# A two-layer hybrid encoder trunk: another order of the output product, low parts and score matmuls issued elsewhere, Fourier matmuls over 128 rows

## The chip, the core and the metric

The kernel runs on one core of a Trainium2 chip. The metric is device time in microseconds of one execution of the whole program. The kernel before was run three times; the time compared is the median. One further execution was recorded by the hardware profiler, and every row quoted here comes from that record. Its columns name the engines as the profile does: PE is the matrix engine, PEld its weight loads, DVE the vector engine, ACT the scalar engine, POOL the engine that issues the accumulating transfers, SP the one that issues the plain loads.

## What is computed

Two layers, each a half-step gated feed-forward block, a mixer of two parallel branches, and a second half-step feed-forward block; a norm at the end. Shapes: 512 tokens, width 1024, inner feed-forward width 2816, 8 heads of 64, all in 32-bit floats.

```
def mixer(h, w_in, gate_bias, rpb, w_na_out, w_f_out, w_o):
    z = h @ w_in                      # q, k, v (512 each), uf (512), ga, gf (1024 each)
    y_na = neighbourhood_attention(q, k, v, rpb) @ w_na_out
    y_f = fourier_mix(uf) @ w_f_out   # real part of a 2-D DFT over positions and channels
    g_na = sigmoid(ga + gate_bias[0])
    g_f = sigmoid(gf + gate_bias[1])
    return (g_na * y_na + g_f * y_f) @ w_o

x = x + 0.5 * swiglu(rms_norm(x, n1), ffn1_w_in, ffn1_w_out)
x = x + mixer(rms_norm(x, nm), ...)
x = x + 0.5 * swiglu(rms_norm(x, n2), ffn2_w_in, ffn2_w_out)
```

Neighbourhood attention works on a grid of 8 rows by 64 columns; a block of 16 query columns sees a band of 32 key columns, so a block's scores are 128 queries by 256 keys.

## The kernel before

**Arithmetic.** Every 32-bit product is made of three passes over rounded parts: high by high, high by low, low by high. A weight tile therefore comes as a raw tile (`raw`, loaded by DMA), a high part (`whi`, made on ACT, line 194 or negated on line 192) and a low part (`wlo`, raw minus high, made on DVE, line 201 or 199). PE takes the two products with `whi` first (lines 351 and 352) and the one with `wlo` last (line 354). Large products are done by a seven-product scheme over 2 by 2 blocks: products m1 to m7 of combined activations with combined weight blocks a, b, c, d. Combined weights are formed in three ways: while a tile is loaded (the POOL queue adds a second block into it, line 155), on DVE (line 187), or, once a tile has served one product, by a POOL transfer that adds another block for the next product (`then`, line 211).

**Stages.** Each layer has a feed-forward stage, a mixer stage and a feed-forward stage. The mixer of layer 1 lies at about 310 to 626 us of the span, that of layer 2 at about 1275 to 1570 us. In the mixer the order of work is written out by hand: on DVE, ACT and PE instructions are issued as the program lists them, from the last part of the feed-forward block before it to the line that closes that regime, ahead of the last gate blocks; behind it, and for the loads throughout, a scheduler that works with estimated times decides the order, unless a call pins an instruction.

**Mixer, in order.** Projections of v and u; q of head pair 0; the Fourier transform over positions (`four_pos`: per 128 output rows six matmuls and one small one, line 1174, that adds the middle row held in `ux`); projections of k and q; then eight attention steps. Step i (`att_step`) does the output of step i-2 (`att_out`), the transposes and splits of step i-1 (`att_trans`, lines 1280 and 359) and the scores of step i (`att_scores`): 12 matmuls of 64 rows on line 1246, two heads at a time, then on DVE the bias and running minimum (line 1255), on ACT the exponentials (line 1262), the division (lines 1268 and 1271). A head pair takes two steps, i even and i odd. Between the steps stand the Fourier transform over channels (`four_ch`, small matmuls on lines 1197 and 1203), projections, and the ten steps of `f_fill` (the Fourier branch's output product; PE tile `ef`, evacuated by ACT and DVE, lines 1362 to 1365, tile `fs`). PSUM has eight banks for all of it, handed out in turn.

From step 5 on the gates' weights are prepared by calls placed by hand: `ws.high()` makes the next item's high part, `ws.low()` the next low part. Then the gate blocks run (`gate_block`, products into A, B, C), with the attention's output product (`n_rows`, PE tile `ps`) between them; `t12` is an activation sum built on DVE in four additions (lines 1555, 1557, 1585, 1589).

**The end of the mixer** multiplies by W_o: seven products into the banks wA, wB, wC, with activation sums m1 to m7 built from the gated branches. The order of products and that of the weights must agree; the latter is `ORDER_W`, line 34. In `strassen`, lines 235 to 242, weights of product 5 then take block a by a POOL transfer, and product 3's are a sum of d and b on DVE. Between the products x is updated (`put`, line 1671) and transposed for the next norm (tile `tr`, line 439).

**The loads.** `Raw.load` issues the plain load on SP and, for a combined tile, the accumulating transfer on POOL. Issue on each queue is in order: a transfer that waits holds those behind it.

Of the kernel before, what the change touches and what calls it, by code (L numbers as in the profile page):

```python
# [14 lines left out]
ALU = mybir.AluOpType  # L15
AX = mybir.AxisListType

P = 128
# [12 lines left out]
AHEAD = 2  # L31
ORDER = (1, 5, 2, 6, 7, 3, 4)
ORDER_0 = (1, 2, 5, 6, 7, 3, 4)
ORDER_W = (5, 1, 2, 6, 7, 3, 4)
FETCH = (8, 4)
BAND = (0, 1, 3, 4)
HALF = T // 2
KC = HALF + 2
# [57 lines left out]
def encoder_kernel(  # L96
# [47 lines left out]
    class Raw:  # L144
# [3 lines left out]
        def load(self, parts=1):  # L148
            if self.t is None:
                self.t = raw_pool[0](self.n)  # L150
                for c in range(0, self.n, self.n // parts):
                    cs = slice(c, c + self.n // parts)
                    nc.sync.dma_start(out=self.t[:, cs], in_=wst[GRAN_AT[self.key]][:, cs])
                if self.plus:
                    G.dma_start(out=self.t, in_=wst[GRAN_AT[self.plus]][:, 0 : self.n], accum_op=ALU.add)  # L155

    class Item:
        def __init__(self, raw, add=None, neg=False, stage=0, parts=1, pieces=1, then=None, minus=None, kept=False):
# [54 lines left out]
    def stage_items():  # L213
        items, st = [], 0

        def add(*a, **k):
            items.append(Item(*a, stage=st, **k))

        made = {}

        def strassen(s, name, idx, sizes, order, dma=False):
            r = made.setdefault((s, name("a"), idx), {}) if dma and len(order) < 7 and order[0] > 2 else {}
            for q, q2 in () if r else (("a", None), ("b", None), ("c", "a"), ("d", "c")):
                r[q] = [
                    Raw((s, name(q), idx, g), n, q2 and (s, name(q2), idx, g)) for g, n in enumerate(sizes)
                ]
            d2 = [Raw((s, name("d"), idx, g), n) for g, n in enumerate(sizes)]
            for m in order:
                for g in range(len(sizes)):
                    a, b, c, d = [r[q][g] for q in "abcd"]  # L230
                    if m == 1:
                        add(a, neg=True)
                    elif m == 2:
                        add(b)
                    elif m == 3:
                        add(d, None if dma and order is not ORDER_W else b)
                    elif m == 4:
                        add(d2[g])
                    elif m == 5:
                        add(d, then=a.key if dma else None)  # L240
                    elif m == 6:
                        add(d, None if dma else a, then=b.key if dma and order is not ORDER_W else None)
                    else:
                        add(c)

        def out_sizes(c):
            return (1024, 512) if c == 0 else (1024, 1024)

        def ffn(s):
            first = not items  # L250
            for g in range(4):
                add(Raw((s, "cl", g)), parts=2 if first and g < 2 else 1, pieces=2 if first and g == 0 else 1)
            for j in range(NB):
                order = (1, 2, 5, 6, 7, 3, 4) if s == (0, 1) and j == 0 else (1, 5, 6, 2, 7, 3, 4)
                strassen(s, lambda q: q, j, (1024, 1024), order)
            for order in ((1,), (2,), (5, 6, 7, 3), (4,)):
                for c in range(3):
                    strassen(s, lambda q: "o" + q, c, out_sizes(c), order)

        for l in range(L):  # L260
            ffn((l, 1))
            st += 1
            s = (l, 0)
            two = (1024, 1024)
            for g in VG:
                add(Raw((s, "v", g)), kept=g == VG[0])
            for g in range(3):
                add(Raw((s, "up", g), UC * len(UK[g]), (s, "uq", g)))
            for g in range(2):
                add(Raw((s, "un", g)), minus=(s, "um", g))  # L270
            for g in range(8):
                add(Raw((s, "qk", g)))
            for i in range(2):
                add(Raw((s, "fp", i), 1024, (s, "fq", i)))
# [12 lines left out]
        return items  # L287
# [676 lines left out]
    def stage_mixer(l, norm, nxt):  # L964
# [199 lines left out]
            return t  # L1164

        def four_pos():
            alt = fc[0:34, C_K : C_K + KC]
            for gp in range(3):
                cs = slice(gp * P, (gp + 1) * P) if gp < 2 else slice(HALF, UC)
                ps = bank()  # L1170
                to = ps[0 : cs.stop - cs.start, 0:KC]
                for b in range(2):
                    mm3(to, ue[b][:, 0, cs], ue[b][:, 1, cs], dfs[:, 0, b, 0:KC], dfs[:, 1, b, 0:KC], b == 0, False)
                PE.matmul(to, ux[0][0:34, cs], alt, start=False, stop=True)
                if gp == 2:
                    cx.append(low_rows(ps, "cx", 32))
                    continue
# [13 lines left out]
        def four_ch():  # L1191
            px = bank()
            for gp in range(2):
                a = fc[:, C_ALT + 4 * gp : C_ALT + 4 * gp + 4]
                for z in range(2):
                    PE.matmul(px[0:4, 0:KC], a, ce[gp][:, z, :], start=gp == 0 and z == 0, stop=False)
            PE.matmul(px[0:4, 0:KC], fc[0:36, C_X4 : C_X4 + 4], cx[0][0:36, 0:KC], start=False, stop=True)
            p64.append(low_rows(px, "p64", 64, (32,)))
            for gp in range(2):
                ps = bank()  # L1200
                to = ps[:, 0:KC]
                mm3(to, fc[:, C_COS : C_COS + P], fc[:, C_COS + P : C_COS + 2 * P], ce[gp][:, 0, :], ce[gp][:, 1, :], True, False)
                PE.matmul(to, fc[0:36, C_X + gp * P : C_X + gp * P + P], cx[0][0:36, 0:KC], start=False, stop=True)
                split(pf[gp][:, 0, :], pf[gp][:, 1, :], to)
                ps = bank()
                to = ps[:, 0:HALF]
# [1 line left out]
                split(qf[gp][:, 0, :], qf[gp][:, 1, :], to)  # L1208

        o, q, k, bms = [], {}, {}, {}  # L1210

        def proj_q(hp):
            q[hp] = hilo("q")
# [14 lines left out]
        def bias_for(hp):  # L1228
            bms[hp] = []
            for e in range(2):  # L1230
                res = mp.tile([P, 3, 256], F32, tag="bm", name=nm("bm"), bufs=4)
                nc.sync.dma_start(out=res, in_=near[l, 2 * hp + e])
                bms[hp].append(res)

        def att_scores(i, after):
            hp, pr = divmod(i, 2)
            (qh, ql), (kh, kl) = q[hp], k[hp]
            ps = [bank(), bank()]
            for jj in range(2):
                j = 2 * pr + jj  # L1240
                ks = slice(BAND[j] * 64, BAND[j] * 64 + 256)
                qs = slice(j * P, (j + 1) * P)
                for i, (a, b) in enumerate(((qh, kh), (qh, kl), (ql, kh))):
                    for e in range(2):
                        r = slice(64 * e, 64 * e + 64)
                        PE.matmul(
                            ps[e][:, jj * 256 : (jj + 1) * 256], a[r, qs], b[r, ks], start=i == 0, stop=i == 2
                        )
            s_ = [tmp(s="s"), tmp(s="s")]
            nmx = sp.tile([P, 4], F32, tag="nmx", name=nm("nmx"), bufs=4)  # L1250
            sm = sp.tile([P, 4], F32, tag="sm", name=nm("sm"), bufs=4)
# [54 lines left out]
                r = slice(64 * e, 64 * e + 64)  # L1306
                V.tensor_tensor(ol[r], pv[e], oh[r].bitcast(F32), ALU.subtract)

        sc, pt_ = {}, {}

        def att_step(i, then=None, before=None, last=None):
            if 0 <= i - 2 < 8:
                att_out(i - 2, pt_.pop(i - 2))
            if then:
                then()
            if 0 <= i - 1 < 8:
                pt_[i - 1] = att_trans(sc.pop(i - 1))
            if before:
                before()
            if i < 8:  # L1320
                sc[i] = att_scores(i, last)

# [201 lines left out]
        for _ in range(4):  # L1524
            next(f_rows)
        ws.high()
        next(f_rows)
        att_step(6, ws.low)
        for _ in range(5):
            next(f_rows)  # L1530
        ws.high()
        att_step(7, ws.low, ws.prep_one)
        next(block)
        ws.high()
        ws.low()
        next(block)
        next(block)
        ws.high()

        B = {(i, j): [z[i].bitcast(F32)[:, :, j * 256 : (j + 1) * 256] for z in (hx, lx)] for i in range(2) for j in range(2)}  # L1540

# [22 lines left out]
            split(hx[0][:, :, 256:512], lx[0][:, :, 256:512], t12)  # L1564

        next(first)
        att_step(8, ws.low)
        next(block)
        next(first)
        t12 = next(first)  # L1570
# [11 lines left out]
        acts[5] = low(h1, t12, "t1")  # L1582
        ws.high()
        ws.low()
        V.tensor_tensor(t12, t12, B[1, 1][0], ALU.add)
        next(block_1)
        ws.high()
        ws.low()
        V.tensor_tensor(t12, t12, B[1, 1][1], ALU.add)
        next(block_1)  # L1590
        h2 = high(t12, "t2")
# [42 lines left out]
        w = [ws.next(), ws.next()]  # L1634
        merge(1, ga1, gf1, w)
        m10, m11 = ga1
        a2 = parts(m10, "m2")
        pb = pair("wB")
        product(pb, a5, K4, True)
        put(pb, 1, 1, -1)  # L1640
        a6 = combo(m00, m00, m11, ALU.add, "m6")
        pa = pair("wA")
        product(pa, a1, K4, True)
        put(pa, 0, 0, -1)
        V.tensor_tensor(m01, m01, m11, ALU.subtract)
        a7 = parts(m01, "m7")
        a3 = parts(m11, "m3")
        pc = pair("wC")
        product(pc, a2, K4, True)
        put(pc, 0, 0, 1)  # L1650
        nxt.squares(0, 0)
        product(pa, a6, K4, False, again=True)
        put(pa, 0, 1, -1)
        a4 = combo(m10, m10, m00, ALU.subtract, "m4")
        product(pa, a7, K4, False, again=True)
        put(pa, 1, 1, 1)
# [232 lines left out]
```

## Time and profile before

| quantity | value |
|---|---|
| median of three runs | 1905.83 us |
| lowest and highest | 1903.82 and 1906.01 us |
| the profiled execution's own time | 1903.99 us |
| its span, first to last instruction | 1902.2 us |
| PE busy in the span | 1874.4 us (99%) |
| DVE, ACT, POOL busy | 1513.3, 1163.3, 172.9 us |
| mean granted PE clock | 0.997 |

The span lies 1.8 us under the execution's time, and that lies 1.84 us under the median of the runs. PE is idle for about 28 us of the span, hence a change can shorten the program either by closing some of this idle time or by making PE's busy work take less. A row of a timeline gives start, duration of one instruction (or of the group), engine, line, operation, output<-input, and in brackets the idle time ahead of it with what ended it. Since PE overlaps neighbouring matmuls, the cost of one is the distance from its start to the next start and not the duration that its row shows.

### The profile page before, as it was taken

What the parts mean: (1) busy time and instruction counts of PE and PEld (TensorE: products, weight loads), DVE (VectorE), ACT (ScalarE), POOL (GpSimd) and SP (SyncE); (2) the same over time, 40 slices, a digit from 0 to 9 for tenths busy, and PEclk for the clock granted to TensorE, in tenths of its full rate; (3) what the DMA queues carried; (4) which work ended last, traced back from release to release, by engine and by line L of the source; (5) the groups of instructions that cost most, each with busy time, mean ns of one, the idle gap of its engine ahead of it and who ended that gap; (6) DMA issues with size and microseconds to landing.
All of it is one profiled execution on the core that took longest, in us unless ns stands there. A gap on an engine that the chain in (4) does not pass through costs nothing.

```text
span 1902.2 us, 25942 instructions
## 1 busy us (share of the span) xinstructions
PE 1874.4 (99%) x9609; PEld 1587.8 (83%) x9609; DVE 1513.3 (80%) x1906; ACT 1163.3 (61%) x1726; POOL 172.9 (9%) x208
## 2 busy tenths in 40 slices
PE   9999999999999999999999999999999999999997
PEld 7888888888997888888888888888889978888886
DVE  8777799757878777779977777996587797776898
ACT  6655665757665655566655556666666566555664
POOL 0101011000110001001000100110002100100010
PEclk9999999999999999999999999999999999999999
DMA  9777588763985577749757764978649965765593
GB/s 290 209 204 189 155 244 272 232 167 119 244 234 146 148 189 203 184 149 265 238 148 200 193 186 150 262 248 250 172 140 219 229 175 140 196 186 158 180 289 122
DMA packets 107726, 376.82 MB, mean 198 GB/s; under 512 B 12224, under 2 KB 12352, under 8 KB 107600
## 3 DMA queue, kind: packets, MB, share of 16 engines
q1 hardware_dynamic: 78944, 275.19, 41.1%
q0 software_dynamic: 28224, 99.68, 28.8%
q8 instruction: 75, 1.23, 0.3%
q14 instruction: 51, 0.42, 0.1%
q10 hardware_dynamic: 432, 0.30, 0.1%
HBM read 368.83 MB, written 6.29 MB: 197 GB/s over the span
## 4 chain that ended last, share of the span: by engine, by line
PE 85%; DVE 6%; ACT 5%; DMA 2%; issue 2%; SPq 0%; ACTq 0%; DVEq 0%
PE A L351 9%; PE A L352 8%; PE A L354 8%; PE o L351 7%; PE o L352 7%; PE o L354 7%; PE B L354 4%; PE B L351 4%; PE B L352 4%; PE ps L354 2%; PE ps L351 2%; PE ps L352 2%; PE tr L593 2%; DMA raw<-in_wst_dram 2%; PE C L354 2%; PE C L351 2%
## 5 line engine op out<-in xcount | busy, mean ns | idle before, releaser
L201 DVE TENSOR_TENSOR wlo<-raw,whi 128x1024 fp32r<-128x1024 f32 (+2 forms) x524 | 620.2, 1192 | 237.1 <-ACT whi L194 235.6
L194 ACT ACTIVATE whi<-raw 128x1024 fp32r<-128x1024 f32 (+2 forms) x524 | 538.2, 1032 | 371.5 <-PE A L352 126.8
L155 POOL DMA_DIRECT2D raw<-in_wst_dram x162 | 140.2, 866 | 1491.1 <-DMA raw<-in_wst_dram 783.9
L187 DVE TENSOR_TENSOR raw<-raw,raw 128x1024 f32<-128x1024 f32 (+1 forms) x132 | 156.8, 1192 | 2.4
L351 PE MATMUL A<-whi,xh 128*128 128x512 f32 x320 | 124.5, 389 | 0.0
L352 PE MATMUL A<-whi,xl 128*128 128x512 f32 x320 | 124.5, 389 | 0.0
L677 ACT ACTIVATE th<-sn,r 128x512 f32<-128x512 f32 x80 | 57.1, 716 | 75.4 <-DVE sn L575 75.4
L199 DVE SCALAR_TENSOR_TENSOR wlo<-raw,whi 128x1024 fp32r<-128x1024 f32 x76 | 90.4, 1192 | 5.5 <-ACT whi L192 5.4
L192 ACT ACTIVATE whi<-raw 128x1024 fp32r<-128x1024 f32 x76 | 78.7, 1036 | 25.8 <-PE o L352 8.5
L354 PE MATMUL A<-wlo,xh 128*128 128x512 f32 x320 | 92.1, 389 | 0.0
L570 ACT ACTIVATE sn<-A 128x512 f32<-128x512 f32 x96 | 56.0, 590 | 43.3 <-PE A L354 43.2
L354 PEld LDWEIGHTS A<-wlo,xh 128*128 128x128 f32 x320 | 60.1, 188 | 12.5
L352 PEld LDWEIGHTS A<-whi,xl 128*128 128x128 f32 x320 | 60.1, 188 | 12.5
L351 PEld LDWEIGHTS A<-whi,xh 128*128 128x128 f32 x320 | 60.1, 188 | 12.5
L351 PE MATMUL B<-whi,t1h 128*128 128x512 f32 x160 | 63.8, 399 | 0.0
L351 PE MATMUL A<-whi,t2h 128*128 128x512 f32 x160 | 62.5, 391 | 0.0
L352 PE MATMUL B<-whi,t1l 128*128 128x512 f32 x160 | 62.4, 390 | 0.0
L351 PE MATMUL A<-whi,t3h 128*128 128x512 f32 x160 | 62.4, 390 | 0.0
L352 PE MATMUL A<-whi,t2l 128*128 128x512 f32 x160 | 62.3, 389 | 0.0
L352 PE MATMUL A<-whi,t3l 128*128 128x512 f32 x160 | 62.3, 389 | 0.0
L351 PE MATMUL B<-whi,xh 128*128 128x512 f32 x160 | 62.3, 389 | 0.0
L351 PE MATMUL C<-whi,xh 128*128 128x512 f32 x160 | 62.2, 389 | 0.0
(431 smaller groups left out, 4910.6 us busy)
## 6 DMA issues: line engine op xcount, KB each, us to landing
raw<-in_wst_dram SPq DMA_DIRECT2D x459, 512.0 KB
raw<-in_wst_dram POOLq DMA_DIRECT2D x176, 512.0 KB, 8.1
raw<-in_wst_dram SPq DMA_DIRECT2D x30, 256.0 KB
vc<-vd SPq DMA_DIRECT2D x28, 256.0 KB
bm<-in_near_dram SPq DMA_DIRECT2D x16, 384.0 KB
vd<-v SPq DMA_DIRECT2D x8, 512.0 KB
dft<-in_dft_dram POOLq DMA_DIRECT2D x4, 514.0 KB, 8.7
x<-in_xin_dram SPq DMA_DIRECT2D x4, 512.0 KB
```

What stands on the lines that cost most here:

```text
L155: G.dma_start(out=self.t, in_=wst[GRAN_AT[self.plus]][:, 0 : self.n], accum_op=ALU.add)
L187: V.tensor_tensor(self.raw.t, self.raw.t, self.add.t, ALU.add)
L192: S.activation(self.out[0][:, cs], self.raw.t[:, cs], AF.Copy, scale=-1.0)
L194: S.activation(self.out[0][:, cs], self.raw.t[:, cs], AF.Copy)
L199: self.last = V.scalar_tensor_tensor(lo, t, -1.0, hi.bitcast(F32), ALU.mult, ALU.subtract)
L201: self.last = V.tensor_tensor(lo, t, hi.bitcast(F32), ALU.subtract)
L351: PE.matmul(ps, lh, rh, start=start, stop=False, skip_group_check=again)
L352: PE.matmul(ps, *((lh, rl) if w == "l" else (ll, rh)), start=False, stop=False, skip_group_check=again)
L354: PE.matmul(ps, *((ll, rh) if w == "l" else (lh, rl)), start=False, stop=stop, skip_group_check=again)
L570: S.activation(t[:, b, :], ps[b], AF.Copy)
L593: PE.transpose(tr[:, k, b * P : (b + 1) * P], a[:, b, (q + k) * P : (q + k + 1) * P], ident)
L677: S.activation(th[:, b, :], g[:, b, :], AF.Silu, scale=norm.r[:, c : c + 1])
```

## The change

Six edits, all in the mixer.

1. `four_pos` and `four_ch`: the matmuls over 34 or 36 rows take all 128 rows. The rows added hold zeros on both sides.
2. The scores' matmuls are taken out of `att_scores` into `att_run(hp)`. It issues those of both steps of a head pair in one run of 24 at the even step, behind the transposes (`SW` is false). Four PSUM banks hold them instead of two.
3. `ws.low()` is called one attention step sooner at steps 6 to 8, and the pair of calls behind step 7 is rearranged to match.
4. The addition of B[1,1][0] to `t12` moves behind the next pair of high and low parts.
5. `ORDER_W` becomes (1, 5, 6, 2, 7, 3, 4), with the products at the end in that order. Weights of product 6 now become d + a by a DVE sum, and those of product 3 take b from a POOL transfer behind product 6; product 5's no longer have one.
6. The accumulating load of the tiles whose key is ("gc", 1, 1) is pinned to its place in the program order.

```diff
-ORDER_W = (5, 1, 2, 6, 7, 3, 4)
+ORDER_W = (1, 5, 6, 2, 7, 3, 4)
@@ Raw.load
-                    G.dma_start(out=self.t, in_=wst[GRAN_AT[self.plus]][:, 0 : self.n], accum_op=ALU.add)
+                    z = G.dma_start(out=self.t, in_=wst[GRAN_AT[self.plus]][:, 0 : self.n], accum_op=ALU.add)
+                    if self.key[1:] == ("gc", 1, 1):
+                        tc.keep_in_program_order(z)
@@ strassen
-                        add(d, None if dma and order is not ORDER_W else b)
+                        add(d, None if dma else b)
...
-                        add(d, then=a.key if dma else None)
+                        add(d, then=a.key if dma and order is not ORDER_W else None)
-                        add(d, None if dma else a, then=b.key if dma and order is not ORDER_W else None)
+                        add(d, None if dma and order is not ORDER_W else a, then=b.key if dma else None)
@@ four_pos, four_ch
-            alt = fc[0:34, C_K : C_K + KC]
+            alt = fc[:, C_K : C_K + KC]
-                PE.matmul(to, ux[0][0:34, cs], alt, start=False, stop=True)
+                PE.matmul(to, ux[0][:, cs], alt, start=False, stop=True)
-            PE.matmul(px[0:4, 0:KC], fc[0:36, C_X4 : C_X4 + 4], cx[0][0:36, 0:KC], start=False, stop=True)
+            PE.matmul(px[0:4, 0:KC], fc[:, C_X4 : C_X4 + 4], cx[0][:, 0:KC], start=False, stop=True)
-                PE.matmul(to, fc[0:36, C_X + gp * P : C_X + gp * P + P], cx[0][0:36, 0:KC], start=False, stop=True)
+                PE.matmul(to, fc[:, C_X + gp * P : C_X + gp * P + P], cx[0][:, 0:KC], start=False, stop=True)
@@ attention
+        SW = False
+        def att_run(hp):
+            (qh, ql), (kh, kl) = q[hp], k[hp]
+            for pr in range(2):
+                ps = sps[2 * hp + pr] = [bank(), bank()]
+                for jj in range(2):
...
+                            PE.matmul(
+                                ps[e][:, jj * 256 : (jj + 1) * 256], a[r, qs], b[r, ks], start=n == 0, stop=n == 2
+                            )
         def att_scores(i, after):
             hp, pr = divmod(i, 2)
-            (qh, ql), (kh, kl) = q[hp], k[hp]
-            ps = [bank(), bank()]
...
+            ps = sps.pop(i)
@@ att_step
+            if SW and i < 8 and not i % 2:
+                att_run(i // 2)
             if 0 <= i - 1 < 8:
                 pt_[i - 1] = att_trans(sc.pop(i - 1))
             if before:
                 before()
+            if not SW and i < 8 and not i % 2:
+                att_run(i // 2)
@@ low parts
         ws.high()
+        ws.low()
         next(f_rows)
-        att_step(6, ws.low)
+        att_step(6)
         for _ in range(5):
             next(f_rows)
         ws.high()
-        att_step(7, ws.low, ws.prep_one)
+        att_step(7, lambda: (ws.low(), ws.prep_one()), None, ws.high)
+        next(block)
+        ws.low()
         next(block)
         ws.high()
+        next(block)
         ws.low()
-        next(block)
-        next(block)
-        ws.high()
...
-        att_step(8, ws.low)
+        att_step(8)
@@ t12
-        V.tensor_tensor(t12, t12, B[1, 1][0], ALU.add)
         next(block_1)
         ws.high()
         ws.low()
+        V.tensor_tensor(t12, t12, B[1, 1][0], ALU.add)
@@ the product with W_o
-        a2 = parts(m10, "m2")
-        pb = pair("wB")
-        product(pb, a5, K4, True)
-        put(pb, 1, 1, -1)
         a6 = combo(m00, m00, m11, ALU.add, "m6")
         pa = pair("wA")
         product(pa, a1, K4, True)
         put(pa, 0, 0, -1)
+        pb = pair("wB")
+        product(pb, a5, K4, True)
+        put(pb, 1, 1, -1)
+        a2 = parts(m10, "m2")
         V.tensor_tensor(m01, m01, m11, ALU.subtract)
         a7 = parts(m01, "m7")
-        a3 = parts(m11, "m3")
+        product(pa, a6, K4, False, again=True)
+        put(pa, 0, 1, -1)
         pc = pair("wC")
         product(pc, a2, K4, True)
         put(pc, 0, 0, 1)
         nxt.squares(0, 0)
-        product(pa, a6, K4, False, again=True)
-        put(pa, 0, 1, -1)
+        a3 = parts(m11, "m3")
```

How it moves instructions, at the three places on which the prediction rests. In the rows a tile's name carries a running number; the numbers of the two programs need not agree, and the lines of the kernel changed are 2 to 12 higher.

First the POOL queue of layer 1 about the second half of the gates. `raw_4712` and `raw_4752` are the tiles of block d of the first gate half, which take another block on line 211 after each use; `raw_5000` is the tile with the key ("gc", 1, 1). Before:

```order
L211 DMA raw_4516<-in_wst_dram 128x1024
L155 DMA raw_5000<-in_wst_dram 128x1024
L211 DMA raw_4712<-in_wst_dram 128x1024
L211 DMA raw_4752<-in_wst_dram 128x1024
L155 DMA raw_5229<-in_wst_dram 128x1024
```

And now:

```order
L213 DMA raw_4516<-in_wst_dram 128x1024
L213 DMA raw_4712<-in_wst_dram 128x1024
L213 DMA raw_4752<-in_wst_dram 128x1024
L155 DMA raw_5000<-in_wst_dram 128x1024
L213 DMA raw_4712<-in_wst_dram 128x1024
```

The two accumulating transfers into the tiles of block d stand ahead of the load of `raw_5000` instead of behind it.

Second, DVE between the last score step (`s_4354`, division on the first row) and the first products of the gates. C's two weight tiles are those whose low parts stand next, `p` is the attention's split, `t_828` the sum `t12`, and `wlo_4635` (now `wlo_4634`) is the low part for which `n_rows` waits. Before:

```order
L1268 TENSOR_TENSOR s_4354<-s_4354,rs_4358 128x512
L201 TENSOR_TENSOR wlo_4401<-raw_4141,whi_4400 128x1024
L1555 TENSOR_TENSOR t_828_4436<-xh_2846 128x1024
L1307 TENSOR_TENSOR o_3998<-ps_4439,o_3998 64x2x8x16 x2
L201 TENSOR_TENSOR wlo_4434<-raw_4295,whi_4433 128x1024
L359 TENSOR_TENSOR p_4462<-ps_4457,p_4462 128x512
...
L201 TENSOR_TENSOR wlo_4603<-raw_4431,whi_4602 128x1024
L1585 TENSOR_TENSOR t_828_4436<-t_828_4436,xh_2802 128x1024
L201 TENSOR_TENSOR wlo_4635<-raw_4501,whi_4634 128x1024
L1589 TENSOR_TENSOR t_828_4436<-t_828_4436,xl_2803 128x1024
```

And now:

```order
L1275 TENSOR_TENSOR s_4354<-s_4354,rs_4358 128x512
L203 TENSOR_TENSOR wlo_4366<-raw_4141,whi_4365 128x1024
L203 TENSOR_TENSOR wlo_4431<-raw_4309,whi_4430 128x1024
L1567 TENSOR_TENSOR t_828_4437<-xh_2846 128x1024
L1314 TENSOR_TENSOR o_4012<-ps_4440,o_4012 64x2x8x16 x2
L361 TENSOR_TENSOR p_4462<-ps_4457,p_4462 128x512
...
L203 TENSOR_TENSOR wlo_4603<-raw_4428,whi_4602 128x1024
L203 TENSOR_TENSOR wlo_4634<-raw_4501,whi_4633 128x1024
L1600 TENSOR_TENSOR t_828_4437<-t_828_4437,xh_2802 128x1024
L1601 TENSOR_TENSOR t_828_4437<-t_828_4437,xl_2803 128x1024
```

The second low part of C has moved ahead of an addition and of the attention's output, and the low part for `n_rows` ahead of an addition to `t12`.

Third, DVE in the product with W_o, layer 1. L187 (now L189) forms a weight sum, L1671 (now L1683) updates x, and m7l, m3l and m4l are low parts of activations. Before:

```order
L359 TENSOR_TENSOR m7l_5635<-sn_4917,m7h_5634 128x1024
L359 TENSOR_TENSOR m3l_5639<-sn_5260,m3h_5638 128x1024
L1671 SCALAR_TENSOR_TENSOR x<-wC_5642,x 128x512
L1671 SCALAR_TENSOR_TENSOR x<-wC_5643,x 128x512
L201 TENSOR_TENSOR wlo_5689<-raw_5477,whi_5688 128x1024
L187 TENSOR_TENSOR raw_5229<-raw_5229,raw_5362 128x1024
L201 TENSOR_TENSOR wlo_5707<-raw_5553,whi_5706 128x1024
```

And now the weight sums stand here:

```order
L361 TENSOR_TENSOR m6l_5547<-sn_4433,m6h_5546 128x1024
L189 TENSOR_TENSOR raw_5292<-raw_5292,raw_5229 128x1024
L1683 SCALAR_TENSOR_TENSOR x<-wA_5550,x 128x512
L1683 SCALAR_TENSOR_TENSOR x<-wA_5551,x 128x512
L189 TENSOR_TENSOR raw_5331<-raw_5331,raw_5262 128x1024
L203 TENSOR_TENSOR wlo_5593<-raw_5292,whi_5592 128x1024
L1683 SCALAR_TENSOR_TENSOR x<-wB_5590,x 128x512
L203 TENSOR_TENSOR wlo_5613<-raw_5331,whi_5612 128x1024
```

The two sums have moved from behind the low parts of m7 and m3 to directly behind the low part of m6, two products earlier.

More of the change, by code (lines that the diff above doesn't have):

```diff
@@ L1233, in bias_for @@
                 bms[hp].append(res)
+        def att_run(hp):
[3 more added lines that the diff above has]
+                for jj in range(2):
+                    j = 2 * pr + jj
+                    ks = slice(BAND[j] * 64, BAND[j] * 64 + 256)
+                    qs = slice(j * P, (j + 1) * P)
+                    for n, (a, b) in enumerate(((qh, kh), (qh, kl), (ql, kh))):
+                        for e in range(2):
+                            r = slice(64 * e, 64 * e + 64)
+                            PE.matmul(
+                                ps[e][:, jj * 256 : (jj + 1) * 256], a[r, qs], b[r, ks], start=n == 0, stop=n == 2
+                            )
         def att_scores(i, after):
             hp, pr = divmod(i, 2)
-            (qh, ql), (kh, kl) = q[hp], k[hp]
-            ps = [bank(), bank()]
[L1239 to L1248, printed above, removed]
+            ps = sps.pop(i)
             s_ = [tmp(s="s"), tmp(s="s")]
@@ L1307, in att_out @@
                 V.tensor_tensor(ol[r], pv[e], oh[r].bitcast(F32), ALU.subtract)
-        sc, pt_ = {}, {}
+        sc, pt_, sps = {}, {}, {}
         def att_step(i, then=None, before=None, last=None):
```

## The prediction

> **What bounds the kernel now.** I read the busy shares first, then the waits of PE, then windows over the mixer, then timelines and the chain of waits about each stall. The page, the table of PE's waits (total, times, longest) and windows (busy time of PE, PEld, DVE, ACT, POOL, then clock, DMA share, GB/s):
>
> ```profile
> PE 1874.4 (99%) x9609; PEld 1587.8 (83%) x9609; DVE 1513.3 (80%) x1906; ACT 1163.3 (61%) x1726; POOL 172.9 (9%) x208
> PE wB L351 <- ACT whi L194: 3.7, 2, 1.9
> PE ef L354 <- DVE wlo L201: 2.9, 2, 1.5
> PE ps L354 <- DVE wlo L201: 1.4, 2, 0.9
> PE C L354 <- DVE wlo L201: 1.2, 2, 0.6
> 540.00:560.00 20.00, 19.56 (x157) 18.85 (x157) 16.62 (x18) 13.40 (x23) 3.54 (x4) 1.00 0.83 233
> 580.00:600.00 20.00, 19.41 (x90) 15.95 (x88) 20.00 (x22) 11.52 (x14) 0.00 (x0) 1.00 0.29 76
> 600.00:620.00 20.00, 18.71 (x79) 15.44 (x80) 17.44 (x20) 14.46 (x25) 1.51 (x2) 0.91 0.73 218
> 640.00:900.00 260.00, 260.00 (x1198) 216.66 (x1197) 202.01 (x204) 154.40 (x196) 21.60 (x25) 1.00 0.67 187
> 1540.00:1560.00 20.00, 18.13 (x88) 14.98 (x87) 18.85 (x20) 14.62 (x28) 1.73 (x2) 1.00 0.64 202
> ```
>
> PE bounds the program. In a feed-forward stage it has no idle time at all (260.00 of 260.00); what can be won lies in the two mixers, in PE's waits (each "2 times" is one per layer) and in matmuls that take longer than their columns. DVE has no gap from 580 to 600, and the clock stood at 0.91 in the window behind that.
>
> **Fourier matmuls.** Timeline of PE; what counts is the distance between starts:
>
> ```profile
> 380.68 0.28 PE L345 MATMUL ps<-dft,ue 128*128 128x258 f32 x1
> 380.80 0.28 PE L346 MATMUL ps<-dft,ue 128*128 128x258 f32 x1
> 381.01 0.38 PE L1174 MATMUL ps<-fc,ux 34*128 34x258 f32 x1
> 381.32 0.39 PE L344 MATMUL ps<-dft,ue 128*128 128x258 f32 x1
> 381.55 0.28 PE L345 MATMUL ps<-dft,ue 128*128 128x258 f32 x1
> ...
> 457.81 0.28 PE L1352 MATMUL ef<-pq,whi 128*128 128x258 f32 x1
> 457.93 0.28 PE L1354 MATMUL ef<-p,w 68*128 68x258 f32 x1
> 458.05 0.41 PE L1357 MATMUL ef<-pq,wlo 128*128 128x258 f32 x2
> ```
>
> Two 128-row matmuls of 258 columns start 0.12 us apart. Into the 34-row one it is 0.21, out of it 0.31, and the next step is 0.23: 0.09 + 0.19 + 0.11 = 0.39 lost about one such matmul, 0.28 if the last part is left off. The 68-row matmul has 0.12 on both sides, though a part of its rows is missing too; so it isn't the missing rows that cost but a change of height that 34 rows bring about and 68 don't. At 128 rows the six matmuls of a layer (three on line 1174, one on 1197, two on 1203) should lose nothing: 6 x 0.28 to 6 x 0.39 is 1.7 to 2.3, I take 2.0 a layer, **4.0 us**. PE has no wait there, so this is won at once, and the ACT and DVE work behind it starts earlier by as much. The added memory rows are zeros that are written already (the tiles are cleared whole), so no other engine gets work.
>
> The Trainium skill ("TensorE: Matmul & The Clock Gate", the section on why this matters for your kernels) says that a matmul over 32 rows takes as long as one over 128. By that alone this part brings 0, and the whole sum below would be 8.0; the distances above speak against it for a low matmul among full ones.
>
> **Scores in one run.**
>
> ```profile
> 406.71 0.98 PE L1246 MATMUL ps<-k,q 64*128 64x256 f32 x12
> 407.62 0.50 PE L351 MATMUL ps<-xh,whi 128*128 128x512 f32 x1
> 407.95 0.39 PE L352 MATMUL ps<-xl,whi 128*128 128x512 f32 x1
> 408.18 0.39 PE L351 MATMUL ps<-xh,whi 128*128 128x512 f32 x1
> ...
> 447.06 1.29 DVE p L359 x2
> 448.35 0.33 DVE s L1255
> 448.72 2.09 ACT s L1262 x8
> ...
> 458.75 2.09 ACT s L1262 x8
> ...
> 455.40 0.28 PE L352 MATMUL ef<-pq,whi 128*128 128x256 f32 x1
> 457.11 0.51 PE L354 MATMUL ef<-pq,wlo 128*128 128x256 f32 x2 [1.43 <-DVE wlo L201]
> ```
>
> A run of 12 (timeline of PE; then four rows of the chain of waits, and PE again) takes 0.91 us to the next matmul, and that one's successor comes 0.33 behind it instead of the 0.23 that follows (407.95 to 408.18): 1.01. Twelve matmuls of 256 columns, two heads side by side, are six times 0.12, or 0.72. Some 0.3 per run goes into changing height; four runs a layer fewer would save up to 4 x 0.3 x 2 = 2.4 us on PE. I count 0 of it. From 415 to 490 the chain of waits runs over DVE and ACT, not PE: the exponentials (448.72, 458.75) come 10.0 us apart, and between them DVE has the same list of instructions after the change as before, in another order. PE only follows there. The same holds for the wait at 457.11 (1.43 us): its low part now comes ahead of two evacuations of the Fourier rows and the wait should go, but the transposes behind it then wait for the division on DVE by so much longer. So 0, with 2 x 1.6 (455.40 to 457.11 less 0.12) as the upper end. The lower end is below nothing: four banks are held, and the step-6 run asks for two more while rows of `ef` are still being evacuated; a wait for one `p` (1.29 for two, row 447.06) a layer costs 1.3.
>
> **Low parts sooner.** C waits twice for the low part that stands behind the division and an addition on DVE. A wait costs 0.16 beyond its bracket (1.71 - 0.12 = 1.59 against 1.43). The order now has both low parts of C's weights first and their high parts one step sooner, so: 1.2 + 2 x 0.16 = **1.5 us**. Bounds 0, if the low part waits for its high part on ACT, and 1.8. The addition to t12, in the chain of waits (start, time on the chain):
>
> ```profile
> 489.13 1.22 DVE t L1585
> 490.35 1.15 DVE wlo L201
> ```
>
> The low part that `n_rows` waits for stands behind the addition of 1.22. With the addition moved behind it, it comes 1.2 sooner, and the waits are 0.5 and 0.9 (1.4 in two): both go, 1.4 + 2 x 0.16 = **1.7 us**. The addition itself is late next by 1.2; behind it stands the high part of t12 on ACT, used some products later. If that cover were gone, 1.2 a layer would come back.
>
> **Transfers.** POOL, the chain of waits (third row), ACT and PE:
>
> ```profile
> 526.78 0.86 POOL L155 DMA_DIRECT2D raw<-in_wst_dram x1 [9.67 <-DVE wlo L201]
> 527.31 2.11 POOL L211 DMA_DIRECT2D raw<-in_wst_dram  x2
> 527.85 15.02 DMA raw<-in_wst_dram
> 539.14 1.06 ACT L194 ACTIVATE whi<-raw 128x1024 fp32r<-128x1024 f32 x1 [3.23 <-DMA raw<-in_wst_dram]
> 547.92 0.39 PE L351 MATMUL A<-t3h,whi 128*128 128x256 f32 x1 [0.40 <-ACT sn L570]
> ```
>
> The two accumulating transfers on line 211 wait behind the load of `raw_5000`, which itself waited 9.67; the chain of waits then goes 15.02 us through the transfer, over ACT's high parts, to small waits of PE (0.44 us in 540 to 560, in three pieces). Ahead of that load they may go as soon as their tiles' low parts are done, which is somewhere in those 9.67; I estimate the middle, 4 to 5 us sooner. POOL then holds `raw_5000` behind them for two issues, about 2.1 us, and what it feeds comes four products later, so that delay is hidden; uncovered it would cost those 2.1. Bracket plus 0.16 a piece is 0.9 in layer 1; **1.2 us** for both, 0 to 2. The larger part of this edit is that the 3.6 us a layer won ahead of it aren't lost here: the transfer's start is set by loads and not by PE, so without it PE would arrive earlier and wait longer.
>
> **The product with W_o.** DVE, PE and the chain of waits:
>
> ```profile
> 598.83 1.23 DVE L187 TENSOR_TENSOR raw<-raw,raw 128x1024 f32<-128x1024 f32 x1
> 601.29 0.58 PE L351 MATMUL wB<-whi,m3h 128*128 128x512 f32 x1 [1.87 <-ACT whi L194]
> 601.87 0.43 PE wB L352
> ```
>
> The weights of m3 are summed on DVE at 598.83, behind all the low parts of the products ahead, then go through ACT, while PE waits 1.87 in each layer (1.87 + 0.16 = 2.03). In layer 1 some eight matmuls behind it are 0.43 apart instead of 0.23 (clock 0.91 in that window): 8 x 0.2 = 1.6; layer 2 has a wait of the same length and clock 1.00. After the change m3's weights come from a POOL transfer that may start when m6's low parts are done, two products ahead of use: a product is 24 matmuls x 0.23 = 5.5 us, so two give 11 us, against 15 us for three transfers in the chain row above, or 10 for two: just enough. The sums for m6 stand two products earlier, but in a stretch where DVE is busy 20.00 of 20; its total work there is the same. So I let half of each wait come back, in pieces of a few tenths behind m6's and m2's low parts: 2 x 2.03 / 2 + 1.6 = **3.6 us**, with 0 and 5.7 as the ends.
>
> The Trainium skill, "TensorE: Matmul & The Clock Gate", the section on HAM oscillation, asks for idle gaps under about 3.4 us, by which 1.87 would not slow the clock; layer 1 shows that it can, layer 2 that it need not. By that rule the 1.6 would be chance, and the sum 10.4.
>
> **Sum.** 4.0 + 1.5 + 1.7 + 1.2 + 3.6 = 12.0 us. The profiled execution would go from 1903.99 to 1892.0. It lies 1.84 under the median of 1905.83, so for the median of runs I forecast 1905.83 - 12.0 = **1893.8 us**.
>
> **Rivals.** (a) *All of it lies on PE.* Then the 2.4 of the scores, the 3.2 of `ef` and the whole of the waits at W_o (2.0 more) come on top: 19.6, 1886.2. For it: PE is 99% busy, so it seems the bound everywhere. Against: in the steps from 415 to 490 the chain is on DVE and ACT. (b) *DVE gives the waits back.* It does the same instructions in 440 to 500 and 580 to 609, so what no longer waits for one low part waits for the next: 1.5 and 1.7 come back, and of W_o only the slow clock's 1.6 is won: 4.0 + 1.2 + 1.6 = 6.8, 1899.0. For it: 20.00 of 20. Against: in 480 to 500 the addition that moves has no PE work waiting for it. (c) *Four banks for the scores.* At each of the four runs a layer PE waits until the step ahead has given back two banks: one pair of `p` (1.29) and the four instructions that read the scores on DVE (0.33 each, row 448.35): 2.6 a run, eight runs, 20.8 against the 12.0: 8.8 slower, 1914.6. It decides from 12.0 / 8 = 1.5 us a run on. Against: at steps 0, 2 and 4 the tiles in between are projections that are evacuated at once. (d) *The change of height isn't it:* 128 rows are no faster, and the sum is 8.0: 1897.8.
>
> **How the numbers follow.** Chances: the forecast 0.57, (a) 0.12, (b) 0.14, (d) 0.07, (c) 0.06, nothing that can be told 0.04. The forecast's own range is 1889 to 1897; with (b) and (d) wholly and the nearer half of (a) inside, 1887 to 1901 leaves out about 0.17. A measurement of this kernel can tell about 0.2%, 3.8 us, from no change. Faster by more than that: the forecast, (a), (d) and most of (b), 0.88; within, 0.06; slower, 0.06.
>
> **What would show it.** Starts 0.12 apart on both sides of the small Fourier matmuls; the exponentials of steps 5 to 7 still 10 us apart; no bracket at C's and `n_rows`' low parts; ACT's high part at about 535 without a DMA bracket; no wait over 1.1 us at W_o and clock 1.00 in both layers. It would be wrong if PE waited at the first matmul of a run of 24 for a bank, or if m3's weights waited for their transfer.

## The result and the profile after

The kernel changed takes 1891.28 us, median of four runs (1888.92 to 1892.29), against 1904.82 us for four runs of the kernel before: 13.5 us less, ratio 0.9929 (95% interval 0.9911 to 0.9946). The forecast was 1893.8 us and 12.0 us less. The profiled execution has a span of 1887.2 us, 15.0 under that of before.

PE's waits (total, times, longest) and windows over the first mixer (PE, PEld, DVE, ACT, POOL busy, clock, DMA share, GB/s) of the kernel changed:

```profile
PE ps L1287 <- DVE s L1275: 3.3, 6, 1.1
PE ps L141 <- ACT warm L138: 3.2, 1, 3.2
PE ef L1362 <- DVE fs L1376: 1.7, 2, 0.9
PE ps L1249 <- DVE fs L1376: 0.6, 2, 0.3
PE o L356 <- DVE wlo L203: 0.5, 1, 0.5
PE A L356 <- DVE wlo L201: 0.5, 2, 0.2
PE wA L356 <- DVE wlo L203: 0.3, 2, 0.2
```

```profile
440.00:460.00 20.00, 17.61 (x150) 16.55 (x148) 15.68 (x42) 14.05 (x42) 0.00 (x0) 1.00 0.22 76
480.00:500.00 20.00, 20.00 (x126) 18.10 (x125) 13.95 (x16) 12.47 (x20) 5.22 (x6) 1.00 1.05 263
540.00:560.00 20.00, 20.00 (x166) 19.81 (x166) 14.98 (x17) 11.75 (x18) 1.75 (x2) 1.00 0.88 238
580.00:600.00 20.00, 19.85 (x90) 15.69 (x89) 20.00 (x22) 12.67 (x16) 1.73 (x2) 1.00 0.75 210
600.00:620.00 20.00, 20.00 (x102) 16.78 (x101) 18.89 (x32) 16.66 (x34) 2.06 (x3) 1.00 0.84 239
```

The waits at wB, C and `n_rows`' low part are gone from the table, and so are those about 545. At W_o a wait of 0.2 per layer is left, and the clock stays at 1.00. DVE still has no gap from 580 to 600. What has grown is the wait of the transposes for the division on DVE (0.9 in all before, now 3.3) and what is new are waits for PSUM banks that DVE has not evacuated yet (`ef` and the scores behind `fs`). Two lines of the kernel before to set beside these:

```profile
PE ps L1280 <- DVE s L1268: 0.9, 4, 0.3
440.00:460.00 20.00, 18.01 (x151) 16.68 (x151) 15.73 (x42) 13.93 (x41) 0.00 (x0) 1.00 0.18 57
```

PE had idle time from 440 to 460 before (18.01 busy of 20), and it still has (17.61).

PE about the first small Fourier matmul, now on line 1176:

```profile
380.72 0.29 PE L348 MATMUL ps<-dft,ue 128*128 128x258 f32 x1
380.85 0.28 PE L1176 MATMUL ps<-fc,ux 128*128 128x258 f32 x1
380.97 0.28 PE L346 MATMUL ps<-dft,ue 128*128 128x258 f32 x1
```

Starts are 0.12 to 0.13 us apart on both sides, where it was 0.21 and 0.31.

**Where the time came from**, by laying the starts of the same matmuls in both traces side by side (time of before less time of the change, us):

| matmul | layer 1 | layer 2 |
|---|---|---|
| first of `four_pos` | 0.07 | 8.67 |
| transposes of step 4 (fifth group) | 2.04 | 10.64 |
| transposes of step 7 (eighth group) | 2.07 | 10.65 |
| C, second weight tile | 3.24 | 11.82 |
| `n_rows`, behind its waits | 4.53 | 13.13 |
| A with t3 | 5.46 | 13.48 |
| next feed-forward stage | 8.63 | 15.09 |

Each mixer first gains 2.0, keeps that through the attention, then gains in four places. Layer 1 gains 3.2 us between the last two rows, layer 2 only 1.6, since layer 1 had the slow clock behind its wait in the trace of before.

### The profile page after: what moved, and what is told of

Its sections match the earlier page's. It is cut to its first block, busy times and chain, and to the rows that moved or that the text cites. A ratio compares the mean times of both kernels' runs of the same rounds, so it can differ in the third digit from the quotient of the medians.

```text
span 1887.2 us, 25961 instructions
## 1 busy us (share of the span) xinstructions
PE 1864.0 (99%) x9609; PEld 1584.7 (84%) x9609; DVE 1511.7 (80%) x1906; ACT 1164.1 (62%) x1726; POOL 172.8 (9%) x208
## 4 chain that ended last, share of the span: by engine, by line
PE 87%; DVE 6%; ACT 4%; issue 2%; DMA 1%; SPq 0%; DVEq 0%; ACTq 0%
PE A L353 9%; PE A L356 9%; PE A L354 9%; PE o L353 7%; PE o L354 7%; PE o L356 7%; PE B L356 4%; PE B L354 4%; PE B L353 4%; PE ps L353 2%; PE ps L354 2%; PE C L356 2%; PE ps L356 2%; PE C L354 2%; PE C L353 2%; PE tr L595 2%
## 5 line engine op out<-in xcount | busy, mean ns | idle before, releaser
L189 DVE TENSOR_TENSOR raw<-raw,raw 128x1024 f32<-128x1024 f32 (+1 forms) x132 | 156.6, 1190 | 2.4
L354 PE MATMUL C<-whi,xl 128*128 128x512 f32 x160 | 62.2, 389 | 0.0
```

The lines of the kernel that those rows point to most:

```text
L189: V.tensor_tensor(self.raw.t, self.raw.t, self.add.t, ALU.add)
L354: PE.matmul(ps, *((lh, rl) if w == "l" else (ll, rh)), start=False, stop=False, skip_group_check=again)
```

## The experiments

All start from the kernel changed; those ahead of the last three undo one thing, wholly or in part. A single span is no good measure of an effect of 1 us: just ahead of a mixer PE waits for a low part of the feed-forward's last product (in the table above the row for o, 0.5). That wait came out between 0 and 2.2 us in the thirteen traces, and in layer 1 it stands ahead of all that the experiments alter. So the effect is read from the traces as in the table above: how much later a matmul of the next feed-forward stage comes than in the trace of the kernel changed, less how much later the first matmul of that layer's `four_pos` comes. Each effect rests on one trace; the two layers agree within 0.25 us in all of them but the kernel with 68 rows.

**Fourier matmuls over 34 and 36, 64, and 68 rows.** The edit, here with 34, in four places:

```diff
-            alt = fc[:, C_K : C_K + KC]
+            alt = fc[0:34, C_K : C_K + KC]
-                PE.matmul(to, ux[0][:, cs], alt, start=False, stop=True)
+                PE.matmul(to, ux[0][0:34, cs], alt, start=False, stop=True)
```

> The changed kernel with the six Fourier matmuls of a layer back at 34 and 36 rows. If leaving the full height costs time (the prediction's first term): starts 0.21 and 0.31 us apart about each of them, the chain of exponentials about 1.9 us later per layer, the span 3.8 to 4.0 us longer than the changed kernel's (about 1891.1 instead of 1887.2). Rival (a matmul over few rows takes what one over 128 takes): 0.12 on both sides and the same span.

> The changed kernel with these six matmuls over 64 rows. If what costs is leaving the full height, 64 rows fall into the same class as 34: 0.28 to 0.39 us lost about each, span 3.8 to 4.0 us longer than 1887.2. If the cost came from the number of rows as such, it would lie between those of 34 and 128 rows, some 2 to 3 us.

> The changed kernel with these six matmuls over 68 rows. If what costs is leaving the full height, 68 rows lose nothing, as the 68-row matmul of the Fourier output product: 0.12 us on both sides, span 1887.2 within 0.3. If the cost came from the number of rows as such, about 2 us longer.

With 34 and 36 rows the layers lose 2.07 and 1.95 us, 4.0 in all (median 1895.03 us; of the span's 7.3 above that of the kernel changed, 3.4 lie ahead of the mixers). With 64 rows 2.02 and 1.93, the same; with 68 rows 0.08 in layer 1. The PE timelines of the kernels with 64 and with 68 rows:

```profile
382.05 0.28 PE L348 MATMUL ps<-dft,ue 128*128 128x258 f32 x1
382.26 0.38 PE L1176 MATMUL ps<-fc,ux 64*128 64x258 f32 x1
382.58 0.39 PE L346 MATMUL ps<-dft,ue 128*128 128x258 f32 x1
```

```profile
380.97 0.29 PE L348 MATMUL ps<-dft,ue 128*128 128x258 f32 x1
381.10 0.28 PE L1176 MATMUL ps<-fc,ux 68*128 68x258 f32 x1
381.22 0.28 PE L346 MATMUL ps<-dft,ue 128*128 128x258 f32 x1
```

At 64 rows the gaps are 0.21 and 0.32, at 68 rows 0.13 and 0.12. So the cost is not in the count of rows: 64 is as dear as 34, and 68 as cheap as 128. In layer 2 the kernel with 68 rows came 1.5 us later between the transposes of steps 4 and 7, far behind the matmuls changed. The windows show why:

```profile
1390.00:1395.00 5.00, 5.00 (x34) 5.00 (x33) 3.41 (x13) 3.27 (x13) 0.00 (x0) 0.72 0.47 182
1395.00:1400.00 5.00, 5.00 (x46) 5.00 (x45) 3.42 (x10) 3.60 (x11) 0.00 (x0) 1.00 0.21 60
```

PE was busy throughout, at a clock of 0.72 for 5 us: a dip of the same kind as that of 600 to 620 in the trace of before, in another place. Its span of 1889.6 contains it.

**Scores in a run per step again.**

```diff
-            if not SW and i < 8 and not i % 2:
-                att_run(i // 2)
+            if i < 8:
+                att_run(i)
```

with `att_run` cut to the 12 matmuls of step i.

> The changed kernel with the scores of each step in a run of their own again, 12 matmuls at each of eight steps, and two banks held. Theory of the prediction (the steps hang on DVE and ACT): span within 0.6 us of 1887.2, the exponentials of steps 5 and 6 still 10 us apart, PE's waits smaller by what the extra runs take. Rival (a) (all of it lies on PE): 2.4 us longer. Rival (c) (waiting for four banks costs): shorter than 1887.2, by the 1.7 + 0.6 us that PE now waits for evacuations.

It is faster by 0.25 us in layer 1 and 0.23 in layer 2 (median 1890.38 us, ratio 0.9921, 0.9906 to 0.9935, which can't be told from the changed kernel's). By the starts in the traces, nothing differs at the transposes of steps 4 and 5 but 0.03, and the gain comes between those of steps 5 and 7. The waits for banks are gone:

```profile
PE o L356 <- DVE wlo L203: 1.8, 1, 1.8
PE ps L1288 <- DVE s L1276: 1.4, 6, 0.3
PE A L356 <- DVE wlo L201: 1.3, 2, 0.7
PE wA L356 <- DVE wlo L203: 0.4, 2, 0.2
```

So the run of 24, part 2 of the change, by itself costs half a microsecond in the two layers together. Its matmuls save PE time where PE waits anyway, and at step 6 it asks for four banks. In the kernel changed the run of step 6 stops at its fourteenth matmul:

```profile
452.47 0.39 PE L1249 MATMUL ps<-k,q 64*128 64x256 f32 x2 [0.30 <-DVE fs L1376]
```

The other three runs of a layer have no such wait. Rival (c) had this mechanism with 2.6 us a run; it is real at one run of four and a tenth of that price. Rival (a) had the kernel changed 2.4 us ahead of this one, and it is behind it.

**Low parts back, t12 back.** The edits are those of the change reversed.

> The changed kernel with the calls for low parts where they were (steps 6 to 8). Theory: C waits 0.6 us twice again and the span is 1.5 to 1.8 us longer than 1887.2; the wait of the Fourier output product for a low part (1.4 us) comes back too, but costs nothing, since the transposes behind it wait as much less. Rival (all of it on PE): 1.5 + 3.2 = 4.7 us longer.

> The changed kernel with the addition to t12 ahead of the low part again. Theory: the output product of the attention waits 0.5 to 0.9 us per layer for that low part; span 1.4 to 1.7 us longer than 1887.2. Rival (the low part would be in time by the room won ahead): same span.

The low parts are worth 1.36 and 1.34 us, 2.7 in all; the addition to t12 0.92 and 0.98, 1.9 in all. PE's waits in the two kernels, low parts back first:

```profile
PE A L356 <- DVE wlo L201: 1.8, 4, 0.6
PE C L356 <- DVE wlo L203: 1.3, 2, 0.6
```

```profile
PE ps L356 <- DVE wlo L203: 1.4, 2, 0.7
```

With the low parts back C waits as it did before, and A waits 1.8 instead of 0.5. The expected wait of `ef` for a low part did not come back: in this kernel there is no wait of `ef` worth a row, neither that one nor the one for banks (1.7). A's waits all lie ahead of the transposes of step 7, and these come no sooner and no later than in the kernel changed. So neither the waits of `ef` nor those of A decide anything there. Of the 1.36, 0.9 come at C, 0.27 between the last transposes and C, and 0.2 behind C. The 0.27 is a wait too short for a bracket. ACT and PE of the kernel with the low parts back:

```profile
473.62 1.04 ACT L196 ACTIVATE whi<-raw 128x1024 fp32r<-128x1024 f32 x1
474.71 0.39 PE L353 MATMUL C<-xh,whi 128*128 128x256 f32 x1
```

C starts as its first high part ends (473.62 + 1.04 = 474.66). The change makes that high part one step sooner, at 465.07, long before C.

**The POOL queue without the pin.**

```diff
-                    if self.key[1:] == ("gc", 1, 1):
+                    if False:
```

> The changed kernel without the pin on the accumulating load, which goes back ahead of the two other transfers on the POOL queue. Theory of the prediction: the transfer's start is set by loads, so PE loses what was won ahead of it: waits of 0.9 us plus up to 3.6 a layer come back, span 2 to 9 us longer than 1887.2. Rival (the loads shift along with PE): only the small waits come back, 1.2 us in both layers.

0.56 and 0.81 us, 1.4 in all. Two timelines of this kernel, POOL and ACT, and then POOL of the kernel changed:

```profile
523.17 0.86 POOL L155 DMA_DIRECT2D raw<-in_wst_dram  x1 [10.41 <-DVE sn L1417]
523.71 2.11 POOL L213 DMA_DIRECT2D raw<-in_wst_dram  x2
```

```profile
534.15 1.06 ACT L196 ACTIVATE whi<-raw 128x1024 fp32r<-128x1024 f32 x1 [2.83 <-DMA raw<-in_wst_dram]
537.94 1.06 ACT L196 ACTIVATE whi<-raw 128x1024 fp32r<-128x1024 f32 x1 [1.93 <-DMA raw<-in_wst_dram]
```

```profile
517.35 0.87 POOL L213 DMA_DIRECT2D raw<-in_wst_dram  x1 [4.81 <-DVE wlo L203]
518.64 0.86 POOL L213 DMA_DIRECT2D raw<-in_wst_dram  x1 [0.42 <-DVE wlo L203]
523.08 0.86 POOL L155 DMA_DIRECT2D raw<-in_wst_dram  x1 [3.58 <-DMA raw<-in_wst_dram]
```

The pin makes the two transfers start about 6 us sooner, and ACT no longer waits for a transfer. But without it the load comes at 523.17, where the kernel before had 526.78: it has moved ahead by 3.6 of the 4.6 us that PE had won by then, and what ended its wait is DVE's work. PE's wait that is back is as small as it was (0.6 in two layers before):

```profile
PE A L353 <- ACT sn L572: 0.7, 2, 0.4
```

So what was won ahead is not lost here. The rival of this experiment holds.

**The product with W_o as before.** `ORDER_W`, the sums in `strassen` and the order of the products, reversed.

> The changed kernel with the product with W_o as before (order of products and weights, and the sums of m3). Theory: PE waits 2.0 us in each layer at m3 again, the waits of 0.2 to 0.3 at m6 go; span 3.2 to 3.6 us longer than 1887.2, and up to 1.6 more in a layer where the clock falls behind the wait. Rival (b) (DVE gives the waits back elsewhere): under 1 us longer but for the clock.

1.26 and 1.32 us, 2.6 in all (median 1895.06 us, ratio 0.9952, 0.9935 to 0.9968). PE in layer 1, and the window about it:

```profile
595.97 0.50 PE L353 MATMUL wB<-whi,m3h 128*128 128x512 f32 x1 [1.87 <-ACT whi L196]
```

```profile
590.00:610.00 20.00, 18.13 (x86) 14.86 (x85) 19.65 (x22) 13.43 (x23) 0.87 (x1) 1.00 0.56 189
```

The same wait of 1.87 is back in both layers, and the clock holds 1.00 in both. Of four such waits seen (two of before, two here), one was followed by a slow clock. Of the 2.03 that the prediction put on each wait, 0.7 to 0.8 come back in the new order; 0.2 of it is the wait at m6 in the table of waits, and the rest was not traced.

**What the attention hangs on.** One more DVE addition of 128x1024 at step 6, between p and the reading of the scores, on a tile that nothing else uses (declared and cleared further ahead):

```diff
-        att_step(6)
+        att_step(6, None, lambda: V.tensor_tensor(dum, dum, dum, ALU.add))
```

> The changed kernel with one more DVE addition of 128x1024 on a tile nobody reads (1.14 us), between the split of p and the reading of the scores at step 6. Theory (from step 2 on the attention steps hang on DVE and ACT, PE follows): everything from step 6 on comes 1.1 us later in each layer, 2.2 us in all. Rival (PE is the bound there): under 0.3 us a layer, inside DVE's idle time.

0.91 and 0.87 us later: about four fifths of the 1.14 us that the addition takes reach the end. DVE, not PE, sets the pace there. Then the other way: three low parts, one in each of steps 5 to 7, put behind the reading of the scores, where DVE would wait for ACT's exponentials. Two of them come out of the stretch between the attention's output and p; the third stood behind the division of step 7.

```diff
-        att_step(5, ws.low)
+        att_step(5, None, None, ws.low)
...
-        att_step(6)
+        att_step(6, None, None, ws.prep_one)
         for _ in range(5):
             next(f_rows)
-        ws.high()
-        att_step(7, lambda: (ws.low(), ws.prep_one()), None, ws.high)
-        next(block)
-        ws.low()
+        att_step(7, ws.prep_one, None, ws.prep_one)
+        next(block)
         next(block)
```

> The changed kernel with three low parts of steps 5 to 7 taken out of the stretch between the attention's output and p and put behind the reading of the scores, where DVE waits for the exponentials anyway. Theory (DVE's list is the chain): the transposes of step 5 and those behind come 1.1 us or more sooner, up to the 2 to 3 us a layer that PE waits there; 2 to 5 us in all. Rival (PE is the bound, or the reciprocals are delayed by as much): within 0.5 us.

> The same with the scores in a run per step, two banks held. Splitting the scores alone was 0.25 us a layer better than the run of 24. If the four banks make PE wait (rival c, in small), this is better than the shadow version alone by 0.2 to 1 us a layer; if PE is the bound once DVE's list is shorter, the four extra runs cost 0.3 each and it is worse by up to 1.2 a layer.

With four banks it is 2.14 and 2.25 us faster than the kernel changed, 4.4 in all; with the scores split 2.57 and 2.62, 5.2 in all. The first has a median of 1887.71 us (ratio to the kernel before 0.9915, 0.9900 to 0.9930), the second 1886.84 us (0.9908, 0.9892 to 0.9925), and it has the lowest median of all kernels here. DVE behind the reading of the scores at step 5, first a row of the kernel changed, then the first of the two:

```profile
448.78 0.17 DVE L1273 RECIPROCAL rs<-sm 128x2 f32<-128x2 f32 x1 [0.82 <-ACT s L1269]
```

```profile
447.11 1.22 DVE L203 TENSOR_TENSOR wlo<-raw,whi 128x1024 fp32r<-128x1024 f32 x1
448.24 0.23 DVE L1273 RECIPROCAL rs<-sm 128x2 f32<-128x2 f32 x2
448.44 0.69 DVE L1275 TENSOR_TENSOR s<-s,rs 128x512 f32<-128x512 f32 x1
```

The low part fills the time in which the second reciprocal waited 0.82 for the exponentials; the division then follows without a gap. PE's waits in the second:

```profile
PE o L356 <- DVE wlo L203: 2.1, 1, 2.1
PE ps L1288 <- DVE s L1276: 1.0, 4, 0.3
PE wA L356 <- DVE wlo L203: 0.3, 2, 0.2
```

The mixers' waits ahead of W_o, 3.3 + 1.7 + 0.6 + 0.5 in the kernel changed, are down to 1.0. Now that PE is nearer to being the bound, the split of the scores still wins, by 0.4 us a layer.

## Why the prediction was right, point by point

- **Fourier, 4.0 us:** measured 4.0, for the reason given. The kernels with 64 and 68 rows show that it is the class of height, and not the count of rows left out.
- **Scores, 0 counted, with 1.3 lost as the lower end and 2.4 for the runs and 3.2 for the wait of `ef` as the upper ends:** measured a loss of 0.5. That the attention hangs on DVE and ACT is shown from both sides (0.9 later with 1.14 more on DVE, 2.2 sooner with low parts moved into DVE's idle time). The wait of `ef` for its low part went; the transposes of step 5 wait 1.05 for the division where it was 0.26, and `ef` now waits for banks. The need for four banks costs a little, as the lower end had it. The sign of being wrong, a wait for a bank at the first matmul of a run of 24, came in small: 0.30 in each layer, at the fourteenth matmul.
- **Low parts, 1.5 us:** measured 2.7, above the upper bound of 1.8. The mechanism was right and the term too small: C's wait with its restart is 0.9 a layer (counted as 0.62 + 0.16), C's start waited another 0.27 for its first high part, which had no bracket and was left out, and 0.2 come behind C.
- **t12, 1.7 us:** measured 1.9, and the waits of `n_rows` come back with the addition, 1.4 in two.
- **Transfers, 1.2 us:** measured 1.4. The clause that went with it fell: that "the transfer's start is set by loads and not by PE, so without it PE would arrive earlier and wait longer". The load ahead of them moved with most of the rest (526.78 to 523.17), so little more was at stake than the small waits.
- **W_o, 3.6 us:** measured 2.6 with an even clock. The 2.0 from the waits was too low, since not half of a wait but about a third came back; the 1.6 for the clock was counted as if the change removed it, while it hung on that execution: with the old order in the new kernel the wait of 1.87 appears twice and no dip.

Rival (b), by which DVE gives the waits back elsewhere, had nothing left of the low parts, of t12 and of W_o's waits; undone, they cost 2.7, 1.9 and 2.6. Of the signs named, the exponentials of steps 5 and 6 are 9.9 us apart (10.0 before), but those of steps 6 and 7 are 11.4; they were 11.2 apart before, so that "10 us" was not true of them from the start.

Summed, the parts undone one at a time give 4.0 - 0.5 + 2.7 + 1.9 + 1.4 + 2.6 = 12.1 us. The two traces, each layer from its first `four_pos` matmul on, give 8.6 + 6.4 = 15.0, or 13.4 without the slow clock of 1.6; so 1.3 us belong to parts that help each other and weren't told apart. The forecast's 12.0 is right in part by balance: without the 1.6 of the clock it held 10.4, and the low parts and W_o's waits were sized too small by 1.2 and 0.6.

By the rule on 32 rows in the Trainium skill, "TensorE: Matmul & The Clock Gate", the section on why this matters for your kernels, the sum would have been 8.0; here a low matmul among full ones costs 0.3 to 0.4 us more. The Trainium skill, "TensorEngine Tiling (Array Packing)", key properties, states a cause that fits: changing the tiling mode drains the engine. What goes on inside the engine no run here shows.

## What to carry to other kernels

Read the distance between starts about the odd small matmul: here one of 34 or 64 rows among those of 128 cost 0.3 us more than its columns say, and padding it with zeros that were there already was free. Before counting a saving on the busiest engine, look where the chain of waits runs in that stretch: 99% busy over the program did not hold for 440 to 490, where an addition on DVE went through by four fifths and grouping PE's matmuls lost 0.25 us a layer. Work with slack belongs into the time in which an engine waits for its partner's answer: here low parts behind the reading of the scores, worth 2.2 us a layer.

## What the runs showed that was not expected

The clock fell behind single waits of PE of about 2 us, in some executions and not in others. At W_o that is one of four waits of 1.87. At the wait ahead of the first mixer (the feed-forward's last product, 0.4 to 2.2 us) the window of 320 to 345 has 0.93 in four of the five kernels in which it lasted 1.8 us or longer, and 1.00 in the fifth. Two of these windows, first of the version with the scores split and the low parts moved (wait 2.1), then of the one with an extra DVE addition (wait 2.0):

```profile
320.00:345.00 25.00, 22.89 (x102) 18.83 (x101) 21.96 (x40) 18.51 (x31) 5.17 (x8) 0.93 0.87 261
```

```profile
320.00:345.00 25.00, 23.00 (x108) 18.36 (x107) 22.18 (x41) 18.84 (x31) 5.19 (x8) 1.00 0.91 276
```

The kernel with 68 rows had its dip behind waits that the kernel changed has too, where it brought none. Each dip is worth about 1.5 us, and the wait ahead of a mixer up to 2.2; between them they could make the 3 us by which runs of one kernel differ, which was not tested. The section on HAM oscillation in the Trainium skill's "TensorE: Matmul & The Clock Gate" names idle gaps of about 3.4 us; the longest single wait ahead of a dip here was 2.2.

A matmul of 64 rows costs as much as one of 34, and one of 68 nothing: the step lies between 64 and 68 rows, and no run here shows where within that.
